# Seven block products in place of eight for 16 of the 44 pairs of up tiles of a two-layer encoder

## The chip, the cores and the metric

The kernel runs on one core of one Trainium2 chip. The metric is the device time of one execution in microseconds (us), lower is better. The engines are PE (TensorE, the matrix products), DVE (VectorE), ACT (ScalarE), POOL (GpSimd) and SP, which here only starts DMAs.

## The reference, cut to what matters

Two requests, of 512 and of 256 tokens, go through two layers that share one set of weights. Each layer is a mixer (attention in three dilated windows, beside a convolution) and a gated feed-forward net, FFN for short. The change is in the FFN.

```python
def conv_ffn(h, w_up, dw_w, w_down):          # h: tokens x 1024
    a, g = jnp.split(h @ w_up, 2, axis=-1)    # w_up: 1024 x 5632
    g = depthwise_conv(g, dw_w)               # 3 taps along the tokens
    return (a * jax.nn.gelu(g)) @ w_down      # w_down: 2816 x 1024
```

The 2816 channels of `a` and of `g` are 22 tiles each of 128 channels. One tile of `a` and the tile of `g` of the same channels are called a pair here; they go into one tile of the hidden layer.

## The kernel before, in words

Activations lie with the channels on the partitions and 768 tokens (512 of the first request, then 256 of the second) along the free axis; 1024 channels are 8 tiles `h_0` to `h_7`. Every float32 operand of a large product is split in a high part (the value rounded to PE's fp32r type) and a low part (what is left), and a product is three matmuls (`three`, L349): weight low by activation high, weight high by activation low, high by high. A tile of up weights (128 x 1024, the contraction's 8 blocks side by side) is thus 8 x 3 matmuls for the 512 tokens and 8 x 3 for the 256, and a pair is 96 matmuls.

The loop of `ffn` (L854) goes through 22 pairs `f`: the product of the `a` tile, the product of the `g` tile, and `hidden` (L858), which gives the other engines this work for each of the two token groups: ACT scales `g` by the middle tap (L865), DVE adds the two other taps (L866, L867), ACT takes gelu (L868), DVE multiplies by `a` (L869). The whole tile is then split: ACT rounds it to `hh` (L870), POOL subtracts for `hl` (L871). DVE reads `g` and `a` from PSUM. The pairs go in chunks of 4, 4, 4, 4, 2 and 4 (`CHUNKS`); after the first pair of a chunk, the tiles of the chunk before are multiplied by their rows of `w_down` (`part`, L449: 192 matmuls for four tiles, called pd) and added to the residual on DVE (L445).

Weights come in one stream of items of 512 KB. `load_ahead` (L230) issues the loads of the next items on SP's queue into 5 raw buffers. `consume` (L298) splits an item: ACT rounds raw to `wh` (L324), ACT writes minus raw, rounded in the same way, into `wl`, and a DMA that accumulates, on POOL's queue, adds raw to it: what is left is the low part. In code, L328 and L329:

```python
nc.scalar.activation(lo, r, AF.Copy, scale=-1.0)
nc.gpsimd.dma_start(out=lo, in_=r, accum_op=ALU.add)
```

The first three items alone have their low part from a subtraction on POOL or DVE (L326). `feed` consumes the next item when a clock of PE's work that the program keeps while it emits (`tick`) has gone on by 1.3 us and fewer than two split items wait; `unit` hands the next split item to a product.

The order of each engine's instructions is the order in which the program emits them. The same clock runs a heap of deferred work (`after`, `run_due`): an emission that should come some time later stands there with its due time, and is emitted when the clock has passed it.

## Time and profile before

| | before |
|---|---|
| median of 3 runs | 1901.37 us (1898.52 to 1904.06) |
| the profiled execution, its own time | 1892.81 us |
| its span, first to last instruction | 1891.0 us |
| mean granted TensorE clock | 0.991 |
| PE / DVE / ACT / POOL busy, share of the span | 97% / 53% / 43% / 19% |
| HBM traffic | 159.83 MB read, 3.18 MB written |

The profile is one execution. Its 1.8 us outside the span lie before the first and after the last instruction. [...] A matmul's own duration in the rows includes its pipeline, so two that follow each other overlap; the distance between their starts (the pitch) is what a matmul costs. The same holds for ACT and DVE in a small measure: the start of the next instruction, not the end of this one, is what counts.

### The profile page before, as it was taken

Reading aid. Unit: us, or ns where it says so; the run is one execution under the profiler, and the core shown is the slowest. Engines: PE = TensorE matmul, PEld = TensorE weight load, DVE = VectorE, ACT = ScalarE, POOL = GpSimd, SP = SyncE. Lnnn points to the kernel's source line nnn. Section 1 sums busy time; section 2 is a strip of 40 time slices with the busy share of each in tenths; the row PEclk is TensorE's granted clock in tenths of the full one; section 3 lists DMA queues with packets and bytes.
Section 4 is the critical chain, followed back from the end, with each engine's and each line's share of the span. In section 5 each row is a group of like instructions: output and inputs, shape, how many; then the busy total and the mean of one; then the engine's idle time right before and its main releaser. Section 6 shows DMA issues by size and latency. Waiting matters only on the chain.

```text
span 1891.0 us, 27649 instructions
## 1 busy us (share of the span) xinstructions
PE 1840.4 (97%) x11164; PEld 1552.1 (82%) x11164; DVE 1000.3 (53%) x1779; ACT 816.8 (43%) x1315; POOL 367.4 (19%) x344
## 2 busy tenths in 40 slices
PE   6999999999999999999999999999899999999999
PEld 4789676778888888888878986768788888888888
DVE  6667666776655655664367886666622221313123
ACT  3324667554423242433343357675543333333331
POOL 1103110033211121211232131100521121211110
PEclk9999999999999999999999999999999999999999
DMA  9666431236667777685635542223457464646454
GB/s 339 176 174 192 122 90 44 67 90 162 184 191 199 212 183 212 156 228 147 145 86 127 124 119 64 65 59 97 93 131 162 106 148 112 149 100 151 101 122 112
DMA packets 80913, 261.81 MB, mean 138 GB/s; under 512 B 9137, under 2 KB 18609, under 8 KB 80785
## 3 DMA queue, kind: packets, MB, share of 16 engines
q0 software_dynamic: 26640, 97.01, 28.4%
q1 hardware_dynamic: 54144, 163.03, 25.4%
q8 instruction: 88, 1.44, 0.3%
q14 instruction: 41, 0.33, 0.1%
HBM read 159.83 MB, written 3.18 MB: 86 GB/s over the span
## 4 chain that ended last, share of the span: by engine, by line
PE 90%; DVE 3%; ACT 2%; issue 2%; DMA 2%; POOL 1%; SPq 0%; POOLq 0%; ACTq 0%; DVEq 0%
PE a L351 6%; PE g L351 6%; PE g L352 6%; PE a L352 6%; PE a L350 6%; PE g L350 6%; PE pd L351 5%; PE pd L352 5%; PE pd L350 5%; PE s L729 4%; PE tp L763 2%; PE o L774 2%; PE v L350 1%; DMA wl<-raw 1%; PE q L350 1%
## 5 line engine op out<-in xcount | busy, mean ns | idle before, releaser
L329 POOL DMA_DIRECT2D wl<-raw x185 | 163.9, 886 | 691.1 <-ACT wl L328 498.0
L324 ACT ACTIVATE wh<-raw 128x1024 fp32r<-128x1024 f32 x188 | 197.2, 1049 | 163.4 <-PE pd L352 69.1
L866 DVE SCALAR_TENSOR_TENSOR gc<-g,fw_sb,gc 128x511 f32<-128x511 f32 x84 | 51.4, 612 | 389.6 <-ACT gc L865 389.6
L558 DVE SCALAR_TENSOR_TENSOR acc<-up,cw_sb,acc 128x783 f32<-128x783 f32 x240 | 246.8, 1028 | 4.3
L328 ACT ACTIVATE wl<-raw 128x1024 fp32r<-128x1024 f32 x185 | 193.4, 1046 | 0.0
L351 PE MATMUL pd<-hl,wh 128*128 128x512 f32 (+1 forms) x576 | 193.2, 335 | 0.0
L352 PE MATMUL pd<-hh,wh 128*128 128x512 f32 (+1 forms) x576 | 192.8, 335 | 0.0
L350 PE MATMUL pd<-hh,wl 128*128 128x512 f32 (+1 forms) x576 | 192.4, 334 | 0.0
L871 POOL TENSOR_TENSOR hl<-gc,hh 128x768 fp32r<-128x768 f32 x44 | 81.8, 1860 | 543.5 <-ACT hh L870 543.5
L865 ACT ACTIVATE gc<-g,fw_sb 128x512 f32<-128x512 f32 x84 | 48.2, 573 | 305.6 <-PE g L352 305.6
L292 DVE CUSTOM_DVE_ANT_0 cro<-raw,cr 128x1024 f32<-128x1024 f32 x112 | 166.6, 1488 | 4.2 <-ACT cr L285 1.5
L445 DVE SCALAR_TENSOR_TENSOR x<-pd,mod,x 128x512 f32<-128x512 f32 (+1 forms) x160 | 96.3, 615 | 133.9 <-PE pd L352 133.9
L350 PEld LDWEIGHTS pd<-hh,wl 128*128 128x128 f32 x576 | 108.1, 188 | 12.3
L351 PEld LDWEIGHTS pd<-hl,wh 128*128 128x128 f32 x576 | 108.3, 188 | 11.7
L352 PEld LDWEIGHTS pd<-hh,wh 128*128 128x128 f32 x576 | 108.2, 188 | 11.4
L868 ACT ACTIVATE gc<-gc 128x512 f32<-128x512 f32 x88 | 46.2, 525 | 130.1 <-DVE gc L867 130.1
L729 PE MATMUL s<-kT,qT 64*128 64x512 f32 (+1 forms) x192 | 94.1, 570 | 0.0
L869 DVE TENSOR_TENSOR gc<-a,gc 128x512 f32<-128x512 f32 x84 | 46.9, 558 | 55.0 <-ACT gc L868 55.0
L741 ACT ACTIVATE sp<-sp,nm 128x512 f32<-128x512 f32 (+1 forms) x96 | 62.1, 647 | 27.5 <-DVE nm L739 24.6
L739 DVE CUSTOM_DVE_ANT_0 sp<-s,G 128x512 f32<-128x512 f32 (+1 forms) x96 | 57.1, 596 | 24.0 <-PE s L729 24.0
L750 ACT ACTIVATE sp<-sp,den 128x512 f32<-128x512 f32 (+1 forms) x96 | 61.8, 645 | 9.0 <-DVE den L748 8.8
L764 ACT ACTIVATE PT<-tp 128x512 f32<-128x512 f32 (+1 forms) x96 | 49.3, 518 | 22.5 <-PE tp L763 21.9
(697 smaller groups left out, 5165.2 us busy)
## 6 DMA issues: line engine op xcount, KB each, us to landing
wl<-raw POOLq DMA_DIRECT2D x185, 512.0 KB, 5.8
raw<-in_w_up SPq DMA_DIRECT2D x88, 512.0 KB, 4.7
raw<-in_wadaT SPq DMA_DIRECT2D x48, 512.0 KB, 5.7
raw<-in_w_down SPq DMA_DIRECT2D x44, 512.0 KB, 4.5
raw<-in_w_in SPq DMA_DIRECT2D x40, 512.0 KB, 4.7
raw<-in_wada SPq DMA_DIRECT2D x24, 512.0 KB, 7.0
raw<-in_w_out SPq DMA_DIRECT2D x16, 512.0 KB, 4.7
G<-bt SPq DMA_DIRECT2D x16, 448.0 KB, 4.5
```

Of the source, the lines that this page charges most:

```text
L292: nc.vector.tensor_tensor_reduce(out=rows["out"], in0=r, in1=rows[g], op0=ALU.mult, op1=ALU.add, scale=1.0, scalar=0.0, accum_out=mod[l][: ...
L324: nc.scalar.activation(hi, r, AF.Copy)
L328: nc.scalar.activation(lo, r, AF.Copy, scale=-1.0)
L329: nc.gpsimd.dma_start(out=lo, in_=r, accum_op=ALU.add)
L350: nc.tensor.matmul(ps, wl, xh, start=first, stop=False)
L351: nc.tensor.matmul(ps, wh, xl, start=False, stop=False)
L352: nc.tensor.matmul(ps, wh, xh, start=False, stop=last)
L445: nc.vector.scalar_tensor_tensor(x[ot][:, span(g)], ps, mod[l][:, gate + ot, g:g + 1], x[ot][:, span(g)], op0=ALU.mult, op1=ALU.add)
L558: nc.vector.scalar_tensor_tensor(a, up[i][:, t:t + ACW], K["cw"][:, l, i, t:t + 1], a, op0=ALU.mult, op1=ALU.add)
L729: nc.tensor.matmul(ps[:, :w], qT[hp][64 * s:64 * s + 64, o + i * P:o + (i + 1) * P], kT[hp][64 * s:64 * s + 64, o:o + w], start=True, stop ...
L741: nc.scalar.activation(sp[:, :w], sp[:, :w], AF.Exp, scale=-1.0, bias=nm, accum_out=den)
L871: nc.gpsimd.tensor_tensor(lo, gc, hi.bitcast(F32), op=ALU.subtract)
```

## The change

In the second layer pairs 6 to 21 are computed by Strassen's scheme in Winograd's form. The two weight tiles of a pair are taken as a 2 x 2 matrix of blocks (rows `a` and `g`; columns: the first four and the last four contraction blocks), and the activations as a 2 x 2 matrix (rows: the first and the last four tiles `h`; columns: tokens 0 to 383 and 384 to 767, `HALF` each). Seven block products of 4 x 3 matmuls, each of 128 x 384, are made in place of eight, 84 matmuls in place of 96. The names of the items: A and G are the raw tiles of `a` and `g`, S the sums A21+A22 and A21+A22-A11, B the block A22, R the differences A11-A21 and A12 minus the second sum. So a pair is split into A (1024 columns), S (1024), B (512) and R (1024), where it was two tiles of 1024.

The three PSUM tiles x, y and z of a pair each get more than one product; copies and sums on ACT and DVE make `av` (the tile of `a`) and `gv` (the tile of `g`) of them in SBUF, and taps, gelu and product then run from SBUF as before (same tap, gelu and split instructions, on SBUF operands). The activation sums are made once, in the background during pairs 1 to 5 (`token_sums`), and the last four of them at pair 6 (`last_sums`), where they are written over the high and low parts of `h_0` to `h_3`, tokens 384 to 767.

The low parts of these 64 items (48 of 1024 columns, 16 of 512) are subtracted on DVE from raw and `wh`; the ACT copy and the accumulating DMA go away for the 32 tiles. The order in which products are emitted is interleaved: a pair's last two products (fifth, sixth) come between the first ones of the next pair.

Emission is by readiness: wrappers of the engines (`V`, `S`, `G`, class `Times`) keep an estimate of when each tile is ready, and `task` puts work into the heap at that time. All instructions of DVE, ACT and POOL therefore have one line, L107, in the changed program. In the rest of the program most of the order stays; for the other items the copy to `wl` and its DMA are emitted 0.8 us of that clock after `wh` (`whole`), not at once.

```diff
+EARLY = 3.0
+NEAR = 0.8
+HALF = NT // 2
+SEVEN = (NF + 1, 6)
+SUMS_FROM = (NF, 1)
...
+    def whole(n, r, hi, lo, freed=1):
+        S.activation(hi, r, AF.Copy)
...
+            def low():
+                if n in open_low:
+                    open_low.remove(n)
+                    S.activation(lo, r, AF.Copy, scale=-1.0)
+                    nc.gpsimd.dma_start(out=lo, in_=r, accum_op=ALU.add)
+                    state["raws"] -= freed
+                    load_ahead()
...
+            after(0.8, low)
...
+    def split(hi, lo, r):
+        return [(lambda: S.activation(hi, r, AF.Copy), (r,)), (lambda: V.tensor_tensor(lo, r, hi.bitcast(F32), op=ALU.subtract), (hi,))]
...
+    def sums(n, r, hi, lo):
...
+            V.tensor_tensor(s[:, :512], g[:, :512], g[:, 512:], op=ALU.add)
+            V.tensor_tensor(s[:, 512:], s[:, :512], a[:, :512], op=ALU.subtract)
...
+    def differences(n, r, hi, lo):
...
+            V.tensor_tensor(g[:, :512], a[:, :512], g[:, :512], op=ALU.subtract)
+            V.tensor_tensor(g[:, 512:], a[:, 512:], s[:, 512:], op=ALU.subtract)
...
+        def last_sums(k=0):
...
+            V.tensor_tensor(t, p[0].bitcast(F32), q[0].bitcast(F32), op=ALU.subtract)
+            V.tensor_tensor(u, p[1].bitcast(F32), q[1].bitcast(F32), op=ALU.subtract)
+            V.tensor_tensor(t, t, u, op=ALU.add)
+
+            def high():
+                S.activation(to[0], t, AF.Copy)
+                waiting.append(task(low, to[0]))
+
+            def low():
+                V.tensor_tensor(to[1], t, to[0].bitcast(F32), op=ALU.subtract)
+                if k < 3:
+                    last_sums(k + 1)
...
+                if f >= SEVEN[l]:
+                    step = seven(f)
+                    step[0]()
+                    if before:
+                        before[2][4]()
+                    step[1]()
+                    if f == SEVEN[l]:
+                        last_sums()
+                    if before:
+                        before[2][5]()
+                    step[2]()
+                    if before:
+                        before[2][6]()
+                        finish(*before[:2], before[2][7])
+                    step[3]()
```

`step[0]` is the first product (A11 by the first block of activations, into x), `step[1]` the second (A12, into y), `step[2]` the third (S, added into x), `step[3]` the fourth part, two products (S into z, and R added into x); `before[2][4]` and `before[2][5]` are the fifth (B, into y) and the sixth (R, added into z) of the pair before.

On PE, before, in pair 15 of the second layer: the `a` tile's product goes from the 512 tokens to the 256 (tiles of PSUM first, then the activation and the weight).

```order
L350 MATMUL a_15_00_15120<-h_7h,wl_14998 128x512
L351 MATMUL a_15_00_15120<-h_7l,wh_14997 128x512
L352 MATMUL a_15_00_15120<-h_7h,wh_14997 128x512
L350 MATMUL a_15_01_15152<-h_0h,wl_14998 128x256
L351 MATMUL a_15_01_15152<-h_0l,wh_14997 128x256
L352 MATMUL a_15_01_15152<-h_0h,wh_14997 128x256
```

On PE, after, in the same pair: the fourth step, where the product by S into z ends and the one by R (`wl_15308`) into x begins; `ts` are the activation sums.

```order
L1164 MATMUL z_15_15264<-ts_2_12754,wl_15209 128x384
L1164 MATMUL z_15_15264<-ts_2_12754,wh_15208 128x384 x2
L1164 MATMUL z_15_15264<-ts_3_12829,wl_15209 128x384
L1164 MATMUL z_15_15264<-ts_3_12829,wh_15208 128x384 x2
L1164 MATMUL x_15_15262<-ts_8_12915,wl_15308 128x384
L1164 MATMUL x_15_15262<-ts_8_12915,wh_15307 128x384 x2
L1164 MATMUL x_15_15262<-ts_9_12964,wl_15308 128x384
```

A matmul of two token groups became one of half the tokens, and the first matmul by R waits for its low part from DVE.

On DVE, before, at the same place: the taps and products of pair 14, and the first of pair 15; nothing of the weights is on this engine.

```order
L866 SCALAR_TENSOR_TENSOR gc_14_15105<-g_14_00_15048,fw_sb,gc_14_15105 128x511
L867 SCALAR_TENSOR_TENSOR gc_14_15105<-g_14_00_15048,fw_sb,gc_14_15105 128x511
L869 TENSOR_TENSOR gc_14_15105<-a_14_00_14991,gc_14_15105 128x512
L866 SCALAR_TENSOR_TENSOR gc_14_15105<-g_14_01_15080,fw_sb,gc_14_15105 128x255
L867 SCALAR_TENSOR_TENSOR gc_14_15105<-g_14_01_15080,fw_sb,gc_14_15105 128x255
L869 TENSOR_TENSOR gc_14_15105<-a_14_01_15023,gc_14_15105 128x256
```

On DVE, after, while PE is in pair 15: one period of the new order. `raw_14980` and `raw_14982` are A and G of pair 15, `raw_15192` and `raw_15194` those of pair 16; `wl_15298` is the low part of B, `wl_15319` that of the next A, `wl_15308` that of R.

```order
L107 TENSOR_TENSOR gv_14_15254<-y_14_15126,gv_14_15254 128x384
L107 TENSOR_TENSOR wl_15298<-raw_14982,wh_15297 128x512
L107 TENSOR_TENSOR raw_14982<-raw_14980,raw_14982 128x512
L107 TENSOR_TENSOR raw_14982<-raw_14980,sum_15210 128x512
L107 TENSOR_TENSOR av_15_15278<-y_15_15263,av_15_15278 128x384
L107 TENSOR_TENSOR wl_15319<-raw_15192,wh_15318 128x1024
L107 TENSOR_TENSOR av_14_15142<-z_14_15127,av_14_15142 128x384
L107 TENSOR_TENSOR sum_15342<-raw_15194 128x512
L107 TENSOR_TENSOR sum_15342<-sum_15342,raw_15192 128x512
L107 TENSOR_TENSOR wl_15308<-raw_14982,wh_15307 128x1024
L107 SCALAR_TENSOR_TENSOR gz_140_15332<-gv_14_15254,fw_sb,gz_140_15332 128x511 x2
```

Between the two tiles' worth of tap work there now stand the low parts, sums and differences of the weights, and among them two instructions that wait for PSUM tiles of PE (y of pair 15, z of pair 14).

On ACT, before, around pair 6 of the second layer: scale and gelu of pair 6, its split, and the splits of two items.

```order
L865 ACTIVATE gc_6_13569<-g_6_00_13512,fw_sb 128x512
L868 ACTIVATE gc_6_13569<-gc_6_13569 128x512
L865 ACTIVATE gc_6_13569<-g_6_01_13544,fw_sb 128x256
L868 ACTIVATE gc_6_13569<-gc_6_13569 128x256
L870 ACTIVATE hh_6_13570<-gc_6_13569 128x768
L324 ACTIVATE wh_13590<-raw_13330 128x1024
L328 ACTIVATE wl_13591<-raw_13330 128x1024
```

On ACT, after, at pair 6, the first by seven products: `h_0h` to `h_3h` are the roundings of `last_sums`, `av_6` and `gv_6` copies of x of pair 6.

```order
L107 ACTIVATE wh_13561<-raw_13304 128x1024
L107 ACTIVATE av_6_13573<-x_6_13555 128x384 x2
L107 ACTIVATE h_0h<-t_13588 128x384
L107 ACTIVATE wh_13597<-sum_13599 128x1024
L107 ACTIVATE gv_6_13644<-x_6_13555 128x384
L107 ACTIVATE h_1h<-t_13626 128x384
L107 ACTIVATE h_2h<-t_13665 128x384
L107 ACTIVATE h_3h<-t_13673 128x384
```

The roundings of the last activation sums stand behind copies of x of pair 6: `h_0h` behind the second copy into `av_6` (after the third product), `h_1h` behind the copy into `gv_6` (after the second part of the fourth).

## Rows read from the trace of the kernel before

**Rows 1.** The page's busy times and chain of waits, whole span.

```profile
PE 1840.4 (97%) x11164; PEld 1552.1 (82%) x11164; DVE 1000.3 (53%) x1779; ACT 816.8 (43%) x1315; POOL 367.4 (19%) x344
...
PE 90%; DVE 3%; ACT 2%; issue 2%; DMA 2%; POOL 1%; SPq 0%; POOLq 0%; ACTq 0%; DVEq 0%
```

**Rows 2.** Windows: a chunk of layer two's FFN: length, busy, clock, DMA share, GB/s.

```profile
1474.20:1572.76 98.56, 98.56 (x579) 86.76 (x578) 23.74 (x40) 34.99 (x44) 17.85 (x16) 1.00 0.55 129
```

**Rows 3.** ACT's timeline, line 865: start, duration, tile, what ended the idle time.

```profile
1474.20 0.69 ACT L865 ACTIVATE gc<-g,fw_sb 128x512 f32<-128x512 f32 x1 [11.71 <-PE g L352]
...
1490.57 0.69 ACT L865 ACTIVATE gc<-g,fw_sb 128x512 f32<-128x512 f32 x1 [6.05 <-PE g L352]
...
1572.76 0.69 ACT L865 ACTIVATE gc<-g,fw_sb 128x512 f32<-128x512 f32 x1 [11.71 <-PE g L352]
```

**Rows 4.** PE's timeline in a down product: the group changes twice.

```profile
1439.70 0.39 PE L350 MATMUL pd<-hh,wl 128*128 128x512 f32 x1
...
1442.45 0.28 PE L350 MATMUL pd<-hh,wl 128*128 128x256 f32 x1
...
1443.81 0.39 PE L350 MATMUL pd<-hh,wl 128*128 128x512 f32 x1
```

**Rows 5.** Groups by form in the chunk of rows 2: busy, mean ns, idle.

```profile
L324 ACT ACTIVATE wh<-raw 128x1024 fp32r<-128x1024 f32 x12 | 12.6, 1049 | 19.3 <-issue 12.5 <-PE pd L352 6.8
...
L871 POOL TENSOR_TENSOR hl<-gc,hh 128x768 fp32r<-128x768 f32 x4 | 7.4, 1848 | 51.5 <-ACT hh L870 51.5
...
L866 DVE SCALAR_TENSOR_TENSOR gc<-g,fw_sb,gc 128x511 f32<-128x511 f32 x4 | 3.0, 749 | 48.6 <-ACT gc L865 48.6
L869 DVE TENSOR_TENSOR gc<-a,gc 128x512 f32<-128x512 f32 x4 | 2.8, 691 | 3.0 <-ACT gc L868 3.0
...
L866 DVE SCALAR_TENSOR_TENSOR gc<-g,fw_sb,gc 128x255 f32<-128x255 f32 x4 | 1.9, 473 | 0.0
...
L869 DVE TENSOR_TENSOR gc<-a,gc 128x256 f32<-128x256 f32 x4 | 1.7, 424 | 2.2 <-ACT gc L868 2.2
```

**Rows 6.** DVE's timeline: one pair's taps and first product.

```profile
1409.16 0.75 DVE L866 SCALAR_TENSOR_TENSOR gc<-g,fw_sb,gc 128x511 f32<-128x511 f32 x1 [11.56 <-ACT gc L865]
1409.94 0.75 DVE L867 SCALAR_TENSOR_TENSOR gc<-g,fw_sb,gc 128x511 f32<-128x511 f32 x1
1411.45 0.69 DVE L869 TENSOR_TENSOR gc<-a,gc 128x512 f32<-128x512 f32 x1 [0.76 <-ACT gc L868]
1412.06 0.47 DVE L866 SCALAR_TENSOR_TENSOR gc<-g,fw_sb,gc 128x255 f32<-128x255 f32 x1
```

**Rows 7.** Timelines of DVE and POOL: a subtraction of 1024 columns on each.

```profile
28.43 2.34 POOL L326 TENSOR_TENSOR wl<-raw,wh 128x1024 fp32r<-128x1024 f32 x1 [3.46 <-ACT wh L324]
...
29.33 2.53 DVE L326 TENSOR_TENSOR wl<-raw,wh 128x1024 fp32r<-128x1024 f32 x1 [1.43 <-ACT wh L324]
```

**Rows 8.** Timelines of POOL and DVE, layer two's second norm.

```profile
1332.39 1.58 POOL L440 TENSOR_TENSOR h_2l<-t,h_2h 128x512 fp32r<-128x512 f32 x1
...
1332.73 1.54 DVE L435 TENSOR_SCALAR t<-t,A,mod 128x512 f32<-128x512 f32 x1
...
1334.90 0.55 DVE L435 TENSOR_SCALAR t<-t,A,mod 128x512 f32<-128x512 f32 x1
...
1336.53 1.45 POOL L440 TENSOR_TENSOR h_4l<-t,h_4h 128x512 fp32r<-128x512 f32 x1
...
1336.78 0.67 DVE L434 TENSOR_TENSOR t<-x,nb 128x512 f32<-128x512 f32 x1
```

**Rows 9.** Windows: PE's idle spell before layer two's FFN, and after it.

```profile
1350.00:1355.00 5.00, 1.95 (x12) 1.38 (x12) 2.88 (x9) 1.24 (x3) 2.18 (x3) 1.00 0.91 208
1355.10:1358.50 3.40, 3.40 (x18) 3.38 (x17) 3.21 (x9) 1.68 (x5) 3.40 (x6) 0.51 0.37 133
```

**Rows 10.** PE's timeline: the FFN's first matmuls in either layer.

```profile
416.81 0.77 PE L350 MATMUL u<-h_0h,wl 128*128 128x512 f32 x1 [3.47 <-DMA wl<-raw]
...
1353.51 0.39 PE L350 MATMUL u<-h_0h,wl 128*128 128x256 f32 x1 [1.41 <-ACT h_0h L438]
```

More of the change, by code (lines that the diff above doesn't have):

```diff
@@ L60, in encoder @@
     ctx.enter_context(tc.manual_schedule())
+    times = Times()
+    V, S, G = (Engine(times, e, n) for e, n in ((nc.vector, "DVE"), (nc.scalar, "ACT"), (nc.gpsimd, "POOL")))
     pool = lambda name, bufs, **k: ctx.enter_context(tc.tile_pool(name=name, bufs=bufs, **k))
@@ L104, in after, with task, run @@
         heapq.heappush(due, (clock[0] + dt, seq[0], fn))
+    def task(fn, *aps):
+        state = []
+        def run():
+            if not state:
+                state.append(1)
+                fn()
+        after(max(times.of(*aps) - clock[0], 0.0), run)
+        return run
     def run_due():
-        while due and due[0][0] <= clock[0]:
+        while due and due[0][0] <= clock[0] + near[0]:
             heapq.heappop(due)[2]()
@@ L121, in tick @@
         clock[0] += dt
+        times.free["PE"] = clock[0]
         run_due()
@@ L325, in consume @@
+        state["raws"] -= 1
+        load_ahead()
+    open_low = set()
+    low_of = {}
+    def whole(n, r, hi, lo, freed=1):
+        S.activation(hi, r, AF.Copy)
         if n < 3:
-            (nc.gpsimd if n < 2 else nc.vector).tensor_tensor(lo, r, hi.bitcast(F32), op=ALU.subtract)
+            (G if n < 2 else V).tensor_tensor(lo, r, hi.bitcast(F32), op=ALU.subtract)
         else:
-            nc.scalar.activation(lo, r, AF.Copy, scale=-1.0)
-            nc.gpsimd.dma_start(out=lo, in_=r, accum_op=ALU.add)
@@ L330, in consume, with in_turn, go, force @@
-        ready.append((hi, lo))
+            def low():
[4 more added lines that the diff above has]
+                    state["raws"] -= freed
+                    load_ahead()
+            open_low.add(n)
+            low_of[n] = low
+            after(0.8, low)
+    def in_turn(n, steps):
+        left = list(steps)
+        def go():
+            if left:
+                left.pop(0)[0]()
+                if left:
+                    after(max(times.of(*left[0][1]) - clock[0], 0.0), go)
+        def force():
+            while left:
+                left.pop(0)[0]()
+        low_of[n] = force
+        go()
@@ L874, in ffn, with finish @@
         f = 0
         pend = []
+        hid = []
+        waiting = []
+        def finish(n, i, last):
+            nonlocal pend, hid
+            nk = CHUNKS[n]
+            if i == (nk if n == len(CHUNKS) - 1 else 1) - 1 and pend:
+                part(l, 40, [h() for h in pend], f"pd{l}_{n}")
+            hid.append(last)
+            if i == nk - 1:
+                pend, hid = hid, []
+        before = None
         for n, nk in enumerate(CHUNKS):
-            hold = nk if n == len(CHUNKS) - 1 else 1
@@ L893, in ffn @@
-            pend = hid
-        last_part(l, 40, pend, f"pe{l}", nxt)
+                if f == SEVEN[l]:
+                    while conv_bg["gen"] is not None:
+                        conv_step(True)
+                    near[0] = NEAR
+                if f == SUMS_FROM[l]:
+                    conv_bg.update(gen=token_sums(), rate=SUMS_RATE[l], acc=0.0)
+                if f >= SEVEN[l]:
[4 more added lines that the diff above has]
+                    step[1]()
+                    if f == SEVEN[l]:
+                        last_sums()
[6 more added lines that the diff above has]
+                    step[3]()
+                    if before:
+                        before[2][7]()
+                    before = (n, i, step)
+                else:
+                    if f == 0:
+                        us = [kslices(unit()) for _ in range(2)]
+                        a, g = product(us, hs, f"u{l}_{f}", key)
+                        release(2)
+                    else:
+                        (a,) = product([kslices(unit())], hs, f"a{l}_{f}")
+                        release()
+                        (g,) = product([kslices(unit())], hs, f"g{l}_{f}")
+                        release()
+                    pair = hidden(f, a, g)
+                    finish(n, i, lambda pair=pair: pair)
@@ L896, in encoder @@
+                f += 1
+        if before:
+            before[2][4]()
+            before[2][5]()
+            before[2][6]()
+            finish(*before[:2], before[2][7])
+        near[0] = 0.0
+        last_part(l, 40, [h() for h in pend], f"pe{l}", nxt)
     first = []
@@ L941, in first_tile @@
         hs[j] = (at(f"h00_{j}h"), at(f"h00_{j}l"))
[L942 removed]
+        modulate(0, 0, j, range(2), hs[j], [rb[:, span(g)] for g in range(2)], V)
     rb0 = first_norm()
```

474 lines of the change are left out of this document (371 added, 103 removed).

## The prediction, made before the change was run

> **What bounds the kernel now.** I read the page's busy times and its chain of waits first [rows 1]: PE is busy 97% of the span, and 90% of the chain that ended last is PE's own work. The reader is to see that little waiting is left: time goes only if PE's work goes. Then the windows over one chunk of the second layer's FFN [rows 2]: PE is busy for all of the 98.56 us at clock 1.00, DVE for 23.74 (24%), ACT for 34.99 (36%). There the other engines have room, and every matmul taken away is time, as long as nobody becomes late. That second half is the question.
>
> The size of a pair comes from the line that starts its tail: the scale of the 512 tokens starts at 1474.20 and, one pair on, at 1490.57; a chunk of four pairs and one down product lasts to 1572.76, 98.56 us [rows 3]. Its 4 x 96 + 192 = 576 matmuls make 0.1711 us each on average, so a pair is 16.42 us.
>
> **What goes: PE.** In a down product 12 matmuls of 512 columns go from 1439.70 to 1442.45, 0.229 us each; 12 of 256 from there to 1443.81, 0.113 each [rows 4]. The cost is proportional to the columns. 384 columns are not in the trace: between 0.113 and 0.229 by these rows. I take the middle, 0.171, since the two lie on one line through zero. Then a product of 12 is 2.05 us, a pair 84 x 0.171 = 14.37, and 16 pairs save 16 x 2.05 = 32.8 us. Were 384 paid as 512, a pair would be 19.2 and the change a loss of 45 us; nothing in the rows has such a step.
>
> **What comes: DVE.** For 384 columns a tensor_tensor is 0.557 us, midway between 0.691 for 512 and 0.424 for 256 [rows 5]; for 1024, on the same line, 1.23. The only subtraction of 1024 columns that DVE made took 2.53 [rows 7], but it began at 29.33 while POOL's of 2.34 had been going since 28.43; POOL's ended at 30.77, and DVE's 1.09 us later. So 1.23 to 2.53 is the bound and 1.23 my value, with the difference kept as a rival below.
> [...]
>
> A pair's DVE work: low parts of A, S and R, 3 x 1.23; of B 0.69; two differences and two sums of 512, 4 x 0.69; four sums from PSUM of 384, 4 x 0.56; taps 2 x 0.75 + 2 x 0.47, products 0.69 + 0.42 [rows 5]: 3.69 + 0.69 + 2.76 + 2.24 + 2.44 + 1.11 = 12.9 us of 14.37. The pitch says a little less: two taps that depend on each other start 0.78 apart for 0.75, but a tap that depends on nothing starts 0.61 after a product of 0.69 [rows 6]. DVE goes from 24% to 85 or 90%, in order, with two instructions in the middle that wait for PE. ACT's splits are four, 3 x 1.05 and one half, where they were four of 1.05 before [rows 5]; with the copies it stays under 60%.
>
> Where is the tightest point? Count from the first matmul of x of pair n, each product 2.05: fifth of the pair before ends at 4.1, second of this at 6.15, sixth of the pair before at 8.2, third at 10.3, first part of the fourth at 12.3; there x needs the low part of R. On DVE, by durations: the sum from y at 4.1 to 4.7, low part of B to 5.4, differences to 6.8, the sum from the next y to 7.4, low part of the next A to 8.6, the sum from z to 9.2, two sums to 10.5, low part of R to 11.8. It is due at 12.3, so 0.5 us to spare (0.8 by pitches). Taps, low part of S and products follow to about 16.5, which is 2.1 in the next pair, and the sum from z to 2.7; DVE then waits for 4.1. In the three pairs with a down product in the middle (9, 13, 17) it has much more room. So in a steady pair I count no wait. The gain stands as long as DVE has 0.5 us.
>
> **The step from the old form to the new.** Count from the first matmul of x of pair 6; no pair before leaves products to it, so third ends at 6.15, the fourth at 10.3, x of pair 7 at 12.3, and then y of pair 6 needs the last activation sums, h_0 to h_3. Each is three DVE operations of 0.56, one ACT rounding (under the 0.69 of 512 columns [rows 3], taken 0.56) and one DVE subtraction. h_0h stands behind the second copy into av_6, thus after 6.15; h_1h behind the copy into gv_6, after 10.3. So h_1h is done at 11.4, its low part at 12.0; each of the two that remain takes 5 x 0.56 and some 0.1 between engines, 2.9: h_3l at 17.8. PE then has its last three matmuls left and ends at 18.3, where it was due at 14.4: 4.0 us. In these 6 us PE does 2 us of work. Before the FFN of this layer a spell like that stands in the trace: 1.95 busy of 5.00 us, then 3.40 us at a granted clock of 0.51, that is at 1.2 GHz, which costs half of them, 1.7 [rows 9]. I take the 1.7 here as well. Behind it, the low part of the next A stands behind pair 6's taps on DVE, which wait for the same y: about 1.65 us more at pair 7. At the other end of the range, nothing: if the chain of sums runs earlier than I think, the 7.35 go.
>
> **The rest.** The activation sums in the background and the DVE work of pairs 1 to 5 lie in an engine that is 24% busy [rows 2]: nothing. The accumulating DMAs of 32 tiles go, from a DMA share of 0.55 [rows 2]: nothing, since PE didn't wait for them in this stretch. Elsewhere the copies to wl and their DMAs come 0.8 us later by the program's own clock. Where a low part came late before, PE stood for 3.47 us at the first layer's FFN, and for 1.41 on h_0h at the second's [rows 10]; either could grow or shrink by as much, so I keep 0 with 3 us to both sides. About 1 us for small waits at pair 21, where no next pair fills the gaps between the last products, and in the down products' pairs.
>
> **Sum.** -32.8 + 4.0 + 1.7 + 1.65 + 1.0 = -24.5 us. The profiled execution took 1892.81 us, its span 1891.0 with 1.8 outside; it becomes 1868.3. The median of the runs stands 8.56 above that execution, and I add it: 1901.37 - 24.5 = 1877 us.
>
> **Rivals.**
> *POOL holds DVE up.* In the norm before this FFN, DVE's tensor_scalar took 1.54 us where the same takes 0.55; it began while POOL's h_2l (1332.39, 1.58 us) was going and ended 0.3 after it, at 1334.27. An operation with one operand in PSUM (1336.78) stayed at 0.67 beside POOL's h_4l [rows 8]. Rows 7 say the same of a subtraction. In the kernel before, DVE's work in the pairs reads PSUM; now the low parts, differences, sums, taps and products are all SBUF to SBUF. POOL's hl still takes 1.85 us a pair [rows 5]. By my walk it starts at about 3.1, after the products at 2.1 and ACT's hh, and is over at 5.0: it catches the low part of B by 0.3 of the 0.5 to spare. If hh comes 2 us later, all the 1.85 fall before the low part of R, and PE waits 1.85 - 0.55 = 1.3 us in each of the 12 pairs after the 6th with no down product: 15.6 us, so 1877 + 15.6 = 1893. For it: the rows. Against it: the 1.4 us that DVE has to itself before the sum at 4.1.
> [...]
>
> [...]
>
> *The transition is hidden.* Sums earlier than by my walk, no fall of the clock, nothing at pair 7: 32.8 less, about 1869.
>
> *It doesn't do what it says.* The order has 84 matmuls in these 16 pairs, so this is only the case of 384 columns at another price; under 1%.
>
> **Chances.** Forecast 0.58; POOL's hold-up 0.20; slower 0.11; hidden transition 0.11. Predicted 1877. Its own range is 1870 to 1884 (3 us elsewhere, the transition's terms, and the spread of the runs). The range is 1864 to 1896: it takes in the hidden transition and POOL's case, and leaves out the slower one. A measurement tells 0.3% from no change, 5.7 us: faster is below 1895.7, slower above 1907.1. Of the forecast's 0.58, 0.55 is faster and 0.03 within; the hidden case is all faster; of POOL's 0.20, 0.13 faster, 0.06 within, 0.01 slower; of the slower case 0.01 is within. So faster 0.55 + 0.11 + 0.13 = 0.79, within 0.10, slower 0.11.
>
> **What would show it.** Matmuls of 384 at a pitch of 0.171. Steady pairs 14.4 us from x to x; no idle time of PE before the first matmul by R; that low part's subtraction at 1.2 us and ending 0.5 us before. If it takes 2 us or more, or its start is late by POOL, the first rival holds. At pair 6, PE idle before y's last matmuls by h_1 to h_3, 4 us in all, released by ACT or DVE. Granted clock 0.5 after that, 1.0 in all other pairs. I am wrong if the FFN's second half shows PE waiting in each pair, or if the mixers change by more than 3 us.

## The result, and the profile after

Four runs of the changed kernel took 1869.22 to 1871.66 us, median 1869.68; four of the kernel before 1898.52 to 1904.06, median 1900.28. The ratio is 0.9838, with a 95% interval from 0.9821 to 0.9856. A later comparison of the same two kernels (six runs against 23) gave 1876.42 against 1893.82, ratio 0.9896, interval 0.9871 to 0.9921. The change is faster in both, by 30.6 us in the one and 17.4 in the other; what can be said of why the two differ follows. The profiled execution took 1871.66 us (span 1869.9), that of before 1892.81, 21.2 more.

The page's busy times and chain of waits, after. They answer to [rows 1]: PE is the bound as before, with 26.5 us less to do, and DVE went from 53% to 63%.

```profile
PE 1813.9 (97%) x10972; PEld 1553.9 (83%) x10972; DVE 1168.7 (63%) x2031; ACT 840.5 (45%) x1379; POOL 342.3 (18%) x312
...
PE 90%; DVE 3%; ACT 2%; issue 2%; DMA 1%; POOL 1%; SPq 0%; ACTq 0%; POOLq 0%; DVEq 0%
```

PE's waits in the changed kernel from the second layer's FFN to the end (what was waited for: us in total, times, longest). In the kernel before, only waits on n111r, h_0h and h_0l stood in this stretch, all of them in front of the FFN's second pair; the same three, 2.8 us, are left out of the lines here.

```profile
PE x L1164 <- DVE wl L107: 1.5, 1, 1.5
PE y L1164 <- ACT h_3h L107: 1.5, 1, 1.5
PE y L1164 <- ACT h_2h L107: 1.5, 1, 1.5
...
PE x L1164 <- ACT av L107: 1.0, 1, 1.0
...
PE y L1164 <- DVE h_3l L107: 0.2, 1, 0.2
PE y L1164 <- DVE h_2l L107: 0.2, 1, 0.2
```

All the waits on x and y are those of the transition. PE's timeline there, start first and the idle time in brackets: x of pair 6 waits for the copy of its first sum, y of pair 6 for h_2 and h_3, x of pair 7 for the low part of R.

```profile
1478.76 0.45 PE L1164 MATMUL x<-ts,wl 128*128 128x384 f32 x1 [1.01 <-ACT av L107]
...
1489.89 0.44 PE L1164 MATMUL y<-h_2h,wl 128*128 128x384 f32 x1 [1.45 <-ACT h_2h L107]
...
1492.56 0.44 PE L1164 MATMUL y<-h_3h,wl 128*128 128x384 f32 x1 [1.47 <-ACT h_3h L107]
...
1505.19 0.45 PE L1164 MATMUL x<-ts,wl 128*128 128x384 f32 x1 [1.49 <-DVE wl L107]
```

Two windows behind these waits, and one of three steady pairs (length, busy times, granted clock, DMA share, GB/s; to be held against [rows 2]). The clock falls for a few us after the stops (0.87 and 0.79 in the two windows), and a product that takes 2.08 elsewhere takes 3.65 (y of pair 7, 1493.61 to 1497.26). In the steady pairs PE is busy throughout at 1.00, with DVE at 34.77 of 43.78, 79%.

```profile
1490.00:1495.00 5.00, 3.22 (x11) 2.40 (x12) 3.56 (x7) 2.09 (x4) 0.00 (x0) 0.87 0.00 0
1495.00:1500.00 5.00, 5.00 (x25) 5.00 (x24) 2.40 (x5) 1.40 (x3) 0.00 (x0) 0.79 0.39 105
...
1569.94:1613.72 43.78, 43.78 (x254) 43.78 (x254) 34.77 (x54) 22.07 (x35) 3.70 (x2) 1.00 0.23 73
```

One steady pair in the changed kernel, pair 11. First PE's timeline: x begins at 1584.53, the first matmul by R is at 1597.04 (12.5 later), and x of the next pair at 1599.12, so a pair is 14.59 us.

```profile
1584.53 0.33 PE L1164 MATMUL x<-h_0h,wl 128*128 128x384 f32 x1
...
1597.04 0.34 PE L1164 MATMUL x<-ts,wl 128*128 128x384 f32 x1
...
1599.12 0.33 PE L1164 MATMUL x<-h_0h,wl 128*128 128x384 f32 x1
```

Then DVE's and POOL's timelines beside it. POOL's hl lies from 3.0 to 4.9 us of the pair; DVE stands idle then, or sums from PSUM (1588.89), and the low part of B begins at 1589.55, when POOL has ended. The low part of R (1594.85, 1.22 us) ends 0.97 us before PE wants it.

```profile
1587.53 1.85 POOL L107 TENSOR_TENSOR hl<-av,hh 128x768 fp32r<-128x768 f32 x1 [40.28 <-ACT hh L107]
...
1588.89 0.56 DVE L107 TENSOR_TENSOR gv<-y,gv 128x384 f32<-128x384 f32 x1 [0.47 <-PE y L1164]
1589.55 0.69 DVE L107 TENSOR_TENSOR wl<-raw,wh 128x512 fp32r<-128x512 f32 x1
...
1594.24 0.69 DVE L107 TENSOR_TENSOR sum<-sum,raw 128x512 f32<-128x512 f32 x1
1594.85 1.22 DVE L107 TENSOR_TENSOR wl<-raw,wh 128x1024 fp32r<-128x1024 f32 x1
```

**A thing in neither argument.** The matmuls that the change doesn't touch do not cost the same in the two profiles. PE's timelines of a down product, 12 matmuls of 256 columns each from the first line to the second; layer one of before, layer one of after, layer two of after:

```profile
612.05 0.28 PE L350 MATMUL pd<-hh,wl 128*128 128x256 f32 x1
...
613.46 0.39 PE L350 MATMUL pd<-hh,wl 128*128 128x512 f32 x1
```

```profile
612.73 0.28 PE L556 MATMUL pd<-hh,wl 128*128 128x256 f32 x1
...
614.09 0.39 PE L556 MATMUL pd<-hh,wl 128*128 128x512 f32 x1
...
1426.13 0.28 PE L556 MATMUL pd<-hh,wl 128*128 128x256 f32 x1
...
1427.54 0.40 PE L556 MATMUL pd<-hh,wl 128*128 128x512 f32 x1
```

1.41, 1.36 and 1.41 us; in layer two of before it was 1.36 [rows 4]. There are two levels, 0.1133 and 0.1177 us a matmul, each kept in these FFNs from the second pair to the last matmul of 256 columns, at a granted clock of 1.00; matmuls of 512 and of 384 columns cost the same beside either. 12 of 512 take 2.75 us at the high level (613.46 to 616.21, layer one of before) and at the low one [rows 4]; 12 of 384 take 2.08 at the high one, and 2.08 right behind columns at the low one (1474.01 to 1476.09, low parts by DMA). The FFN from the second pair's first matmul to the last part's (first `a` to first `pe`) is 499.20 us in layer one of before and 492.81 in layer two: 6.39 us for the level alone. The FFN of before was high in layer one and low in layer two; that of after was low, then high.

### The profile page after: what moved, and what is told of

Same layout as the page of the kernel before. It is cut to its first block, busy times and chain, and to the rows that moved or that the text cites. A ratio compares the mean times of both kernels' runs of the same rounds, so it can differ in the third digit from the quotient of the medians.

```text
span 1869.9 us, 27511 instructions
## 1 busy us (share of the span) xinstructions
PE 1813.9 (97%) x10972; PEld 1553.9 (83%) x10972; DVE 1168.7 (63%) x2031; ACT 840.5 (45%) x1379; POOL 342.3 (18%) x312
## 3 DMA queue, kind: packets, MB, share of 16 engines
q8 instruction: 86, 1.41, 0.3%
## 4 chain that ended last, share of the span: by engine, by line
PE 90%; DVE 3%; ACT 2%; issue 2%; DMA 1%; POOL 1%; SPq 0%; ACTq 0%; POOLq 0%; DVEq 0%
PE pd L557 5%; PE pd L558 5%; PE pd L556 5%; PE x L1164 5%; PE s L935 4%; PE a L558 4%; PE a L557 4%; PE a L556 4%; PE g L558 4%; PE g L557 4%; PE g L556 4%; PE y L1164 3%; PE z L1164 3%; PE o L980 2%; PE tp L969 2%
## 5 line engine op out<-in xcount | busy, mean ns | idle before, releaser
L107 ACT ACTIVATE wh<-raw 128x1024 fp32r<-128x1024 f32 (+1 forms) x204 | 206.4, 1018 | 185.9 <-PE pd L558 61.9
L466 POOL DMA_DIRECT2D wl<-raw x153 | 134.9, 883 | 630.5 <-ACT wl L107 443.4
L107 DVE SCALAR_TENSOR_TENSOR acc<-up,cw_sb,acc 128x783 f32<-128x783 f32 x240 | 246.8, 1028 | 4.3
L107 DVE CUSTOM_DVE_ANT_0 cro<-raw,cr 128x1024 f32<-128x1024 f32 x112 | 166.6, 1487 | 4.2 <-ACT cr L107 1.6
L107 ACT ACTIVATE wl<-raw 128x1024 fp32r<-128x1024 f32 x153 | 160.1, 1047 | 0.0
L107 DVE SCALAR_TENSOR_TENSOR x<-pd,mod,x 128x512 f32<-128x512 f32 (+1 forms) x160 | 95.4, 615 | 102.0 <-PE pd L558 102.0
L107 DVE SCALAR_TENSOR_TENSOR gc<-g,fw_sb,gc 128x511 f32<-128x511 f32 (+1 forms) x104 | 63.9, 614 | 148.5 <-ACT gc L107 146.7
L558 PEld LDWEIGHTS pd<-hh,wh 128*128 128x128 f32 x576 | 108.2, 188 | 11.5
L107 POOL TENSOR_TENSOR hl<-gc,hh 128x768 fp32r<-128x768 f32 x28 | 52.6, 1877 | 338.9 <-ACT hh L107 338.9
L107 ACT ACTIVATE gc<-g,fw_sb 128x512 f32<-128x512 f32 (+1 forms) x52 | 29.8, 574 | 163.9 <-PE g L558 163.9
L107 ACT ACTIVATE sp<-sp,nm 128x512 f32<-128x512 f32 (+1 forms) x96 | 62.1, 647 | 26.0 <-DVE nm L107 23.1
L107 DVE CUSTOM_DVE_ANT_0 sp<-s,G 128x512 f32<-128x512 f32 (+1 forms) x96 | 57.2, 597 | 26.2 <-PE s L935 26.2
L107 DVE TENSOR_TENSOR wl<-raw,wh 128x1024 fp32r<-128x1024 f32 (+1 forms) x49 | 53.2, 1090 | 25.2 <-ACT wh L107 24.3
L107 POOL TENSOR_TENSOR hl<-av,hh 128x768 fp32r<-128x768 f32 x16 | 30.2, 1890 | 211.1 <-ACT hh L107 174.7
L107 ACT ACTIVATE gc<-gc 128x512 f32<-128x512 f32 (+1 forms) x56 | 29.4, 525 | 81.4 <-DVE gc L107 81.4
L107 ACT ACTIVATE sp<-sp,den 128x512 f32<-128x512 f32 (+1 forms) x96 | 61.8, 645 | 7.9 <-DVE den L107 7.6
```

The source lines that it names most:

```text
L107: r = f(*args, **kw)
L558: nc.tensor.matmul(ps, wh, xh, start=False, stop=last)
```

## The experiments

**The kernel before, unchanged, once more.**

> The kernel before, once more. In its profile the first layer's FFN ran its 256-column matmuls at a pitch of 0.1177 us and the second layer's at 0.1133; in the changed kernel it was the other way round, though these matmuls are the same. 1584 matmuls of 256 columns a layer make that about 7 us a layer. Theory: the pitch is a state of one execution, taken up anew where PE's clock returns from 1.2 GHz, so this profile can show another pair of pitches than the first, and the time goes with it (about 1886, 1893 or 1900 us for none, one or both layers at 0.1177). Rival: it belongs to the program (its order, its addresses), so the profile shows 0.1177 and 0.1133 again, and the times stay at 1898.5 to 1904 with one profile at 1893 by another cause.

The profile took 1890.85 us, with the levels the other way round: layer one low, layer two high. The FFNs took 492.81 and 499.20 us, the same two numbers, swapped. The runs went from 1890.85 to 1906.4, those of before on the same chip from 1885.13 to 1907.0. So the level of an FFN is not the program's; it belongs to an execution and a stretch of it.

**The changed kernel, unchanged, once more.**

> The changed kernel, once more. Theory (a state of one execution): the pitches of the two layers may differ from 0.1133 and 0.1177 in the first profile; with both layers at one level the time would be about 1865 (both low) or 1878 (both high). Rival (a property of the program): 0.1133 and 0.1177 again, 1869 to 1872 us each time. Either way PE waits about 5.7 us at pairs 6 and 7, and nowhere in the pairs 8 to 21.

Both FFNs high, and 1876.10 us (runs from 1874.34 to 1877.57), where the first profile, with layer one low, took 1871.66. Layer one's FFN was 500.29 here and 492.81 there; the whole is only 4.4 us apart, since the part in front of that FFN's second pair took 3.1 us less here (442.61 against 445.70). The waits at pairs 6 and 7 were the same to 0.1 us, and pairs 8 to 21 had none again. The high level has two forms: pairs by eight products take 16.64 us (FFN 499.20) or 16.67 (500.29), against 16.43 at the low one (492.81). Where the second layer's FFN began with pairs of 16.64 us the changed kernel took 475.98 (here) and the kernel before 499.20, 23.2 us less; where it began with 16.67, 476.23 (first profile) and 500.29 (eight products throughout, the run with the emission alone below), 24.1 less. Where it began low the worth is smaller: the run with the four stops, which adds nothing in layer two, began there with pairs of 16.43 us and took 475.46, which is 17.4 less than 492.81. A pair by seven products takes 14.59 us in all three, so it saves 1.84 us against a low pair and 2.05 or 2.08 against a high one.

**The last sums made in the background.**

> The changed kernel with the three DVE operations of each of the last four activation sums moved into the background of pairs 1 to 5; only their rounding and low part are left for pair 6. Theory (the chain of sums on DVE and ACT makes y of pair 6 late, and that makes the rest): the waits on h_2, h_3 (3.2 us), the fall of the clock behind them (1.7 us) and the wait of x of pair 7 (1.5 us) go, the wait of 1.0 on the copy of av_6 stays: 6.4 us faster than the changed kernel at the same pitches. Rival (DVE has too much to do at pair 6 in any order): the 6.7 us of sums come out of a stretch in which DVE is free, but another item becomes late, and less than 3 us are gained.

```diff
+            for k in range(4):
+                t = fourth[k] = tmp(f"t4{l}{k}", False)[:, :HALF]
+                p, q = column(k + 4, 0), blocks[1, k]
+                V.tensor_tensor(t, p[0].bitcast(F32), q[0].bitcast(F32), op=ALU.subtract)
+                yield 1
...
+            for k in range(4):
+                S.activation(column(k, 1)[0], fourth[k], AF.Copy)
+                waiting.append(task(lambda k=k: low(k), column(k, 1)[0]))
```

1870.27 us in the profile (runs 1863.46 to 1873.02, median 1870.96), both FFNs high, 5.8 less than the changed kernel once more. The second FFN took 468.51, against 475.98, 7.5 less; the parts ahead of it, which the edit leaves alone, took 1.6 more in this execution. On the chip that ran both, the slowest run of this version is faster than the fastest of the changed kernel. Of the waits of the transition the one on the copy of av_6 is left, as PE's timeline shows:

```profile
1485.07 0.44 PE L1165 MATMUL x<-ts,wl 128*128 128x384 f32 x1 [1.00 <-ACT av L107]
```

The theory holds. It is the fastest version of those that ran on that chip: 0.9862 of the kernel before (0.9831 to 0.9892), the changed kernel 0.9896.

**Emission by readiness alone.**

> The changed program with eight products in all 44 pairs and the low parts by ACT and DMA throughout, so only emission by readiness and the later copy to the low part are left of the change. Theory (the gain is the seven products' alone): the time of the kernel before within 3 us at the same pitches, 1893 to 1902. Rival (the emission gives a part of the 30 us between the medians): 5 us or more faster than before, with shorter waits in the mixers.

```diff
-SEVEN = (NF + 1, 6)
-SUMS_FROM = (NF, 1)
+SEVEN = (NF + 1, NF + 1)
+SUMS_FROM = (NF, NF)
```

Median 1900.19 against 1893.82, ratio 1.0021 (1.0001 to 1.0041): no gain. Its profile had both FFNs high and took 1901.17; the FFN of layer two took 500.29. From the first FFN's last part to the second's second pair it needed 418.08 us. The kernel before needed 419.56 in one profile and 418.06 in the other, the changed kernel 418.19 and 418.47: executions of one kernel differ there by more than the kernels do, and no effect of the emission shows.

**More work on DVE: two operations, then five.**

> The changed kernel with two more DVE operations of 512 columns (1.2 us by the pitch of 0.61) in each of the 16 pairs, in front of the differences (they write the second sum of the weights again, same values). Theory (DVE has room: in the changed kernel's tightest pairs the low part of R ends 0.97 us before PE wants it, in the others about 1.6): PE waits 0.2 to 0.5 us in the three or four tightest pairs and nowhere else, 1 to 2 us in all. Rival (a wait in every pair, with the clock behind it): DVE late in 12 pairs and a fall of the clock after each, 10 us or more.

> The same with five more operations (3.05 us a pair), more than the 2.7 to 3.0 us that DVE stands idle in a pair of the changed kernel. Theory (the end of the low part of R sets it, by simple arrears): PE waits 1.4 to 2.1 us in each of the 12 pairs without a down product, 17 to 25 us in all, and the clock stays at 2.4 GHz, because PE still works for 14 of 16 us. Rival (each wait brings the clock down, 1.7 us more a pair as after the idle spell in front of the FFN): 37 to 45 us, with granted clock about 0.9 in these pairs.

```diff
+            for _ in range(2):        # 5 in the other
+                nc.vector.tensor_tensor(s[:, 512:], s[:, :512], a[:, :512], op=ALU.subtract)
             V.tensor_tensor(g[:, :512], a[:, :512], g[:, :512], op=ALU.subtract)
```

Two operations take 1.40 us. PE waits in three pairs (11, 15 and 19), 3.9 us in all, and the stretch from pair 6 to the last part is 4.9 longer than in the changed kernel, not 1 to 2. One of the waits:

```profile
1603.81 0.42 PE L1166 MATMUL x<-ts,wl 128*128 128x384 f32 x1 [1.27 <-DVE wl L107]
```

In pair 11 the sum from y, which begins 0.2 us after PE has gone on to the next product in the changed kernel, began 1.2 us after it here: DVE carried arrears over from the pair before. So the 0.97 us to spare cannot be spent anew in every pair. The granted clock from 1600 to 1605 us, around this wait, is 1.00. The median is 1879.78 us, 0.9913 of before (0.9884 to 0.9942).

Five operations take 3.59 us, more than I reckoned, and the stretch is 38.3 us longer. PE waits 24.5 us more than in the changed kernel; the rest, 13.8 us, I put down to the fall of the clock, an estimate by difference. It does not fall behind every wait. Behind 1.23 us (1591.82) it stays at 1.00, which the expectation calls 2.4 GHz; behind 4.12 us it goes down, to 0.60 from 1611 to 1617 us:

```profile
1610.82 0.66 PE L1166 MATMUL x<-ts,wl 128*128 128x384 f32 x1 [4.12 <-DVE wl L107]
```

```profile
1591.00:1606.00 15.00, 14.18 (x81) 14.18 (x82) 13.36 (x21) 5.95 (x10) 1.86 (x1) 1.00 0.11 43
1611.00:1617.00 6.00, 6.00 (x23) 6.00 (x24) 4.60 (x8) 2.27 (x4) 0.88 (x1) 0.60 0.30 90
```

The size is the rival's (37 to 45), the mechanism lies between: simple arrears, and a fall of the clock once in a chunk, at the longest wait (4.1 us three times, and 3.4 in the last pair). At 1915.65 us this kernel is slower than before (1.0108, 1.0062 to 1.0154).

**POOL's subtraction made twice.**

> The changed kernel with POOL's subtraction for hl made twice in each of the 16 pairs (same values), so that POOL is at work for 3.7 us from 2.4 to 6.1 us of a pair, not 1.85. Theory (while POOL works, a DVE operation with both operands in SBUF waits until it ends; in the changed kernel POOL's 1.85 us lie where DVE stands idle or reads PSUM): the low part of B (0.69 us, at 5.0 us of a pair) takes about 1.75 us, the low part of R ends 1.1 us later, just late in the three or four tightest pairs: 1 us or less in all, while the sum from y before it stays at 0.56. Rival (no such hold-up; the 2.53 and 2.00 us were something else): the low part of B stays at 0.69 us.

```diff
                 G.tensor_tensor(lo, o["av"], hi.bitcast(F32), op=ALU.subtract)
+                nc.gpsimd.tensor_tensor(lo, o["av"], hi.bitcast(F32), op=ALU.subtract)
```

The timelines of POOL and DVE in pair 11 (the pair begins a little later here):

```profile
1591.91 1.85 POOL L107 TENSOR_TENSOR hl<-av,hh 128x768 fp32r<-128x768 f32 x1 [38.34 <-ACT hh L107]
...
1593.27 0.56 DVE L107 TENSOR_TENSOR gv<-y,gv 128x384 f32<-128x384 f32 x1 [0.47 <-PE y L1164]
...
1593.85 1.86 POOL L1219 TENSOR_TENSOR hl<-av,hh 128x768 fp32r<-128x768 f32 x1
...
1593.94 2.32 DVE L107 TENSOR_TENSOR wl<-raw,wh 128x512 fp32r<-128x512 f32 x1
```

The low part of B began 0.09 us after POOL's second operation and ended at 1596.26, 0.55 after POOL's end: 2.32 us in place of 0.69. The sum with an operand in PSUM stays at 0.56 while the first one is going. Of the 15 pairs whose B is in the trace, B's low part took 2.3 to 2.4 us in four, and the difference behind it 2.3 in three; in the other eight neither took over 0.7. PE waits 0.5 to 0.6 us in four places, 2.4 in all, and the stretch is 3.1 us longer, where 1 or less was expected (median 1876.1 us, 0.9914 of before, 0.9883 to 0.9946). The hold-up is real, and the changed kernel is spared it by where hl falls: in its pairs 8 to 21 every DVE operation in the trace took the time of its form alone (0.69 us for each low part of B, 1.21 to 1.23 for each of 1024 columns). In one place it was not: at pair 6 a low part of 1024 columns took 2.00 us beside POOL's last hl of the old kind.

**Four stops of PE in the first layer's FFN.**

> The changed kernel with ACT kept busy for 23 us (one rounding of weights repeated 24 times) at four places of the first layer's FFN, so that PE runs out of weights there and stops for some us, its clock falls and comes back. Theory (the pitch of 256 columns, 0.1133 or 0.1177 us, is taken up anew when the clock has come back): the pitch changes at one or more of the four stops and nowhere else in the FFN. Rival (it belongs to the layer's stretch of the program or to the execution as a whole): one pitch from the first pair to the last, across all four stops.

```diff
     def whole(n, r, hi, lo, freed=1):
         S.activation(hi, r, AF.Copy)
+        if n in (36, 52, 68, 84):
+            for _ in range(24):
+                nc.scalar.activation(hi, r, AF.Copy)
```

PE stopped four times, for 20.3, 20.6, 8.4 and 20.6 us (one run, 1944.3 us). Behind the first stop, for instance, the granted clock was 0.50:

```profile
511.50:514.00 2.50, 2.50 (x6) 2.02 (x7) 1.92 (x5) 0.72 (x2) 0.00 (x0) 0.50 1.03 175
```

The 256-column matmuls in PE's timeline, in pairs of lines: 24 of them from the first line to the second, before the first stop, then 12 from one to the other after each of the first three stops, and 24 after the fourth:

```profile
479.91 0.28 PE L559 MATMUL a<-h_0h,wl 128*128 128x256 f32 x1
...
482.73 0.39 PE L559 MATMUL g<-h_0h,wl 128*128 128x512 f32 x1
...
532.61 0.28 PE L559 MATMUL pd<-hh,wl 128*128 128x256 f32 x1
...
533.97 0.39 PE L559 MATMUL pd<-hh,wl 128*128 128x512 f32 x1
...
670.07 0.28 PE L559 MATMUL pd<-hh,wl 128*128 128x256 f32 x1
...
671.48 0.40 PE L559 MATMUL pd<-hh,wl 128*128 128x512 f32 x1
...
862.89 0.28 PE L559 MATMUL pd<-hh,wl 128*128 128x256 f32 x1
...
864.25 0.39 PE L559 MATMUL pd<-hh,wl 128*128 128x512 f32 x1
...
970.00 0.28 PE L559 MATMUL a<-h_0h,wl 128*128 128x256 f32 x1
...
972.83 0.39 PE L559 MATMUL g<-h_0h,wl 128*128 128x512 f32 x1
```

2.82 us for 24 matmuls (0.1175), then 1.36 (0.1133), 1.41 (0.1175) and 1.36 (0.1133) for 12, and 2.83 (0.1179) for 24: high, low, high, low, high. The level changed at each of the four stops and nowhere between them.

**Low parts by DMA.**

> The changed kernel with the low parts of A, S and R (the items of 1024 columns) made as before, by an ACT copy and an accumulating DMA; only B's stays on DVE. Theory (the low parts had to go to DVE because a DMA lands 5.9 us after its issue): the differences of R end at about 6.6 us of a pair, wh at 7.7, the copy at 8.7, and the low part lands at 14.5 or later, 2 us or more after PE wants it (12.5): a wait of 2 us or more in most of the 12 pairs without a down product, 25 us or more in all, a large part of the gain gone. Rival (the low parts' way is of no weight, DVE is relieved by 3.7 us a pair and the differences come that much earlier): no wait, the time of the changed kernel.

```diff
+    def by_dma(lo, r):
+        S.activation(lo, r, AF.Copy, scale=-1.0)
+        nc.gpsimd.dma_start(out=lo, in_=r, accum_op=ALU.add)
...
+        if _width(lo) > 512:
+            return [(lambda: S.activation(hi, r, AF.Copy), (r,)), (lambda: by_dma(lo, r), (hi,))]
```

1965.48 us, 1.0381 of before (1.0347 to 1.0415). The waits on x: 68.5 us in 13 places, most of them put down to the copy into av on ACT:

```profile
PE x L1170 <- ACT av L107: 58.8, 11, 8.5
PE x L1170 <- DMA wl<-raw: 9.7, 2, 5.2
```

What made that copy late stands in the timelines of DVE and ACT ahead of one of these waits (PE's, of 5.57 us, ended at 1599.97):

```profile
1596.97 0.69 DVE L107 TENSOR_TENSOR sum<-raw 128x512 f32<-128x512 f32 x1 [6.17 <-DMA wl<-raw]
...
1598.48 1.06 ACT L107 ACTIVATE wh<-sum 128x1024 fp32r<-128x1024 f32 x1 [4.84 <-DVE sum L107]
1599.44 0.47 ACT L107 ACTIVATE av<-x 128x384 f32<-128x384 f32 x1
```

The sum of the next pair is written into a raw buffer, and in this kernel an accumulating DMA still reads such a buffer when the sum's turn comes: DVE stood 6.0 to 9.1 us until the DMA had landed. The rounding of the sum waits for it on ACT, and the copy into av stands behind the rounding. So it is before ten of the eleven copies, 57.7 of the 58.8 us. The theory has the sign and the DMA's landing right, but by way of the buffer and not of PE's own wait for the low part, and far too small a size (it said 25 or more): the waits are 63.6 us more than in the changed kernel, and the stretch is 88.6 us longer. Behind the wait above, from 1600 to 1605 us, the granted clock was 0.50.

**Seven products from pair 4, and in the first layer.**

> As the kernel with the last sums in the background (1870 us with its 256-column matmuls at 0.1177 us), but with seven products from pair 4 on, 18 of 22 pairs, and the background sums emitted at 1.25 of PE's clock, not 0.75. Theory (a pair is worth 16.64 less 7 x 2.08 = 2.07 us wherever the sums are there in time): 4.1 us less, about 1866 at the same pitches. Rival (DVE is too full in pairs 1 to 3): the sums aren't done at pair 4, PE waits more than 4 us there, and nothing is gained.

> As the kernel with seven products from pair 4 of the second layer, and pairs 18 to 21 of the first layer by seven products too. Theory: four pairs more, 8.3 us, less a transition with a wait of 1 us: 7 us less than the kernel from pair 4 on, about 1859 at the same pitches. Rival (in the first layer DVE is at 52 to 62% with the condition's products, of 1.49 us each, before the change, so that with 12.9 us a pair more it is over 100% and the sums of the weights and of the activations come late): PE waits 2 us or more in these pairs or in front of them, no gain or a loss.

```diff
-SEVEN = (NF + 1, 6)
+SEVEN = (NF + 1, 4)               # (18, 4) in the other, with SUMS_FROM = (12, 1)
-SUMS_RATE = (0.6, 0.75)
+SUMS_RATE = (0.6, 1.25)
```

Both on top of the version with the sums in the background. From pair 4: 1895.54 us, 0.9999 of before (0.9975 to 1.0022), the gain gone. PE's waits from layer one's end on, and a window in the first of them:

```profile
PE x L1165 <- DVE wl L107: 24.6, 7, 15.3
```

```profile
1410.00:1420.00 10.00, 2.19 (x20) 1.99 (x18) 9.72 (x15) 2.29 (x4) 2.33 (x1) 0.83 0.00 0
```

DVE is full (9.72 of 10 us) with sums and taps, and the low part of pair 4's A stands behind them: PE waits 15.3 us. The rest of the 24.6 are waits of 0.7 to 3.0 us in later pairs, which the kernel from pair 6 on has not; what makes them late there was not taken apart. With pairs 18 to 21 of the first layer as well it is 1927.76 us (1.0182, 1.0151 to 1.0213): in the first layer one wait of 11.3 us on the copy into av at the change-over and four on low parts, 6.4 us in all, and in the second 26.2 us on low parts, much as from pair 4. The mixer between the two is 16.3 us longer than in the kernel from pair 4, which was not taken apart. Both rivals hold. Of the places tried, DVE has the room only with the start at pair 6 and in the second layer alone.

## Why the prediction was right, and where its steps were off

The forecast was 24.5 us less, and 1877 us. Against a high FFN the changed stretch gives 23.2 or 24.1 us, against a low one 17.4, and the runs lie at 1869.22 to 1877.57.

*Seven for eight.* 384 columns cost 0.1733 us, not 0.171: a product is 2.08 us, a pair 14.59, where I had 14.37. Against the 16.42 of [rows 3] a pair would save 1.8 and not 2.05; against the same layer at the high level (16.64) it saves 2.05. The sum of 32.8 came out against that level (16 x 16.64 - 112 x 2.087 = 32.5), and this is luck: the profile that I worked from had this FFN low, where 16 x 1.84 = 29.4 us is all that the pairs give, and two errors, the price of 384 columns and the level, cancelled.

*DVE in a steady pair.* Right, and the closest step: the low part of R ends 11.5 us into the pair, by the pitch as in the working, with PE wanting it at 12.5. The load was put too high, at 85 or 90%, and is 79%: in the rows of pair 11 an operation of 0.69 us is followed 0.6 us after its start by the next. The order of one pair was taken for all, too: in pairs 8 to 10, 12 to 14, 16 to 18 and 20 the sums stand behind R's low part, and only in 7, 11, 15 and 19, as in the walk, ahead of it. The wait that two more operations brought came in one pair of each chunk, 11, 15 and 19.

*POOL.* hl was put from 3.1 to 5.0 and lies from 3.0 to 4.9. The rival's mechanism is shown by the doubled operation, its condition was not met: beside POOL's second subtraction the low part of B took 2.32 us in place of 0.69 and ended 0.55 after it, and the sum with an operand in PSUM stayed at 0.56 beside the first. Not every one was held up: B's low part took 2.3 to 2.4 us in four of 15 pairs.

*The transition.* 7.35 us were foretold; the 24 products from pair 6 to the first down product take 59.04 us where 24 x 2.085 are 50.0: 9.0. The waits on h_2 and h_3 are 3.2 (4.0 foretold), the clock 1.6 (1.7), the wait at pair 7 1.5 (1.65); it is R's low part that stands behind pair 6's taps, not the next A's, as I had written. Not foreseen: 1.0 on the copy into av_6, which stands behind the end of pair 5 on ACT, and some 1.6 us in slower matmuls around the stops. The version with the sums in the background took 7.5 us of the 9 away. What the trace of before has for the 1.2 GHz of the working is 256 columns every 0.214 us at a granted clock of 0.50 (1356.02 to 1358.37), 1.2 columns a ns.

*Small waits.* 1 us was set aside, and 0.3 came, at pair 21.

*Elsewhere.* 0 with 3 us to both sides. The second mixer shows no difference beyond that between executions of one kernel (418.2 and 418.5 us after, 419.6 and 418.1 before). The part ahead of the first FFN's second pair took 445.7 and 442.6 us after, 442.9 and 442.0 before: within the 3 us, or nearly, and as far apart in one kernel as between the two.

*What failed* is the last line of the sum: "The median of the runs stands 8.56 above that execution, and I add it". I took this for a fixed distance of the profiled execution from the runs. It is not fixed: the second profile of the kernel before lay 4.95 us below the median of its runs, and the runs spread from 1885 to 1907. The levels are worth 6.4 to 7.5 us in each FFN, and the profile had one of two high; that they make the spread is likely but not shown, since the runs between have no profile, and two FFNs give 15 us at most (the mixers have the levels too, as the table below shows). The medians of four runs then differ by 30.6 us, those of 6 and 23 by 17.4, for one and the same change.

## What to carry to other kernels

Fewer matmuls were worth their full time here only while the engine that feeds them had slack in every period: two operations more a pair on DVE, 1.40 us, cost 4.9 us, and five, 3.59, cost 38.3. Read the slack pair by pair at the instruction that PE waits for, and count arrears from the period before. Where a new scheme starts, prepare its first inputs while the old one still runs: that alone was 7.5 us of the FFN here. Before two executions are compared, compare the pitch of a matmul that the change doesn't touch: it made 6.4 to 7.5 us an FFN here.

## What the runs showed of the hardware that was not expected

In these profiles a TensorE matmul of 256 columns (fp32r, new weights each time) started every 0.1133 us or about every 0.1177 at a granted clock of 1.00. Means over 20 us of PE's timeline in nine of the profiles, worked out from the starts of the rows (of the last FFN those ahead of pair 6):

| profile | FFN, layer one | early products of the mixer, layer two | FFN, layer two |
|---|---|---|---|
| before | 0.1175 | 0.1179 | 0.1133 |
| after | 0.1133 | 0.1179 | 0.1177 |
| before, once more | 0.1133 | 0.1133 | 0.1179 |
| after, once more | 0.1180 | 0.1179 | 0.1175 |
| sums in the background | 0.1177 | 0.1133 | 0.1177 |
| emission alone | 0.1175 | 0.1133 | 0.1179 |
| two more on DVE | 0.1178 | 0.1133 | 0.1175 |
| five more on DVE | 0.1179 | 0.1133 | 0.1133 |
| hl twice | 0.1176 | 0.1179 | 0.1177 |

Inside the FFNs the level changed at all four stops made for it. At the transition of pair 6 it went from 0.1133 to 0.118 in the three profiles that came to it low (four stops, five operations more, low parts by DMA), and 0.1177 stayed as it was in the others; behind pair 6 no profile of a kernel by seven products has it low. At the four stops PE had stood for 8.4 to 20.6 us, and behind the first two the clock was at 0.50 (511.5 to 514.0 and 665.6 to 669.0 us) and back at 1.00 from 669 to 680; at the transition with the low parts by DMA, behind a wait of 4.45 us (1504.11), 384 columns started every 0.32 us in place of 0.173. But the level also changed without a fall of the clock. In the run from pair 4 on it went from 0.1179 (1383.42 us) to 0.1133 (1409.31) at a granted clock of 1.00, with no wait of PE above 0.24 us. And in the mixers it changes so too, in the changed kernel's second one for instance, with 108 matmuls from the first line to the second and 60 from the third to the fourth:

```profile
1070.07 0.28 PE L556 MATMUL q<-wh,h_0l 128*128 128x256 f32 x1
...
1082.79 0.38 PE L902 MATMUL hb<-ident,hn 128*128 128x128 f32 x2
...
1089.13 0.28 PE L556 MATMUL k<-wh,h_0l 128*128 128x256 f32 x1
...
1095.93 0.38 PE L902 MATMUL hb<-ident,hn 128*128 128x128 f32 x2
```

That is 0.1178 and then 0.1133 us, at a granted clock of 1.00 from 1053 to 1096 us and without a wait of PE between. What decides the level stays open, and so does whether a program can choose it.
